# A hybrid two-layer block on one core: a fourth raw weight buffer, a deeper weight queue and a reordered mixer

## The chip, the cores and the metric

The kernel runs on one core of a Trainium2 chip. The metric is the device time of one execution in microseconds (us). Before the change it is 1276.12 us, the median of 3 runs (1275.52 to 1276.19).

## The reference

Two layers, each of them a feed-forward block, a mixer block and a second feed-forward block on 256 tokens of width 1024, all in float32, and a last norm:

```python
for l in range(DEPTH):                                   # 2 layers
    x = x + 0.5 * swiglu_ffn(rms_norm(x, ffn1_norm[l]), ffn1_w1[l], ffn1_w2[l])   # 1024 -> 2*2816 -> 1024
    h = rms_norm(x, mix_norm[l])
    proj = h @ w_in[l]                                   # split into gm_u, gm_v, r_q .. r_g, n_q, n_kv, n_g
    y_a = gmlp_mixer(gelu(gm_u), gelu(gm_v), ...)        # layer norm, causal 128x128 mix over tokens
    y_b = retention_mixer(r_q, r_k, r_v, r_g, ...)       # 4 heads, decayed scores, group norm, silu gate
    y_c = nsa_mixer(n_q, n_kv, n_g, ...)                 # compressed, selected and window attention, 8 heads
    g_a, g_b, g_c = split(sigmoid(h @ w_merge_gate[l] + b_merge_gate[l]), 3)
    x = x + (g_a * (y_a @ w_branch_out[l, 0]) + g_b * (y_b @ w_branch_out[l, 1])
             + g_c * (y_c @ w_branch_out[l, 2])) @ w_o[l]
    x = x + 0.5 * swiglu_ffn(rms_norm(x, ffn2_norm[l]), ffn2_w1[l], ffn2_w2[l])
return rms_norm(x, final_norm)
```

## The kernel before

**Weights.** All weights lie in one DRAM tensor in the order of their use and come as pieces of at most 128 x 1024 floats (512 KB). `issue` (L197) makes a piece: a DMA on SyncE's queue (SP) into one of three `raw` buffers (L199), a cast on ScalarE (ACT) to the high half `hl` (L210), and a subtraction that makes the low half (L214) on VectorE (DVE), of which GpSimd (POOL) takes the last part, as `pool_lo` says. `hl` has four buffers. `piece` (L220) hands a piece to TensorE (PE) and issues those up to `AHEAD` = 2 pieces further on. Each product is made of three matmuls: high by high, high by low, low by high.

**Order.** PE's order is the program's. The other engines and SP each have a queue in order, which the framework's scheduler fills from the program by its own model of time. Side work (norms, attention, retention, the gated MLP) is written as generators: `yield 3.5` means "go on when 3.5 us of modelled matmul time have passed on PE", `yield has("vr")` means "go on when this has been emitted". `run_sides` looks at them after every third matmul or so.

**Start.** `ffn` of layer 0 loads x in quarters, each followed by a quarter of the first piece (`xload`, L425). `norm_tile` makes the high half of x on ACT (L314) and the low half on DVE (L315). `square` sums the squares on POOL (L323, L329, L333). `gate_pool` (L250) holds POOL back until a piece is split. `norm_end` (L349) has PE sum over partitions (after `WAIT_FIRST` = 16.5), POOL take the power (L346), and PE spread the result, R, over the partitions; the outputs of the first four column blocks wait in PSUM for R (L398), two of them in the two `mm` banks.

**Mixer.** `feat` and `tok` run through w_in: compressed keys, keys (`f_k`), values, queries (`f_q`), retention's queries and keys, gv, retention's values (`f_vr`, evacuated by ACT at L949), gate features u and g. From `f_q` on, `pool_lo` = 5: POOL makes 3/8 of each low half. `f_q` writes the queries' high half with ACT and their low half with DVE into `ql` (L935), and two DMAs on SP (L937, L938) move that to the other 64 partitions. `mirror` (L532) does the same for keys with two DMAs on SP (L536, L537). `hidden` runs a compression piece of 8 short matmuls between the query and retention blocks. `retention` (L741) makes decayed scores, waits for `vr` and `cmp`, then 1.5, and makes the second stage (L757 on): scores by values, of which the third and fourth head need the second half of `f_vr`. `gmlp` (L837) and `unit` (L616, attention of one query tile and key group) follow as sides. `loads` (L465) brings the mixer's constants, on SP.

Of the kernel before, what the change touches and what calls it, by code (L numbers as in the profile page):

```python
# [7 lines left out]
F32 = mybir.dt.float32  # L8
# [17 lines left out]
AHEAD = 2  # L26
# [12 lines left out]
WAIT_FIRST = 16.5  # L39
# [3 lines left out]
WAIT_SCORE = 4.5  # L43
WAIT_PT = 3.5
WAIT_CB = 8.0
WAIT_GN = 3.5
WAIT_LN = 6.0
WAIT_GMLP = 10.0
# [12 lines left out]
def tile_hybrid_block(  # L61
# [26 lines left out]
    const.tile([128, 24], F32, tag="align", name="align")  # L88
# [36 lines left out]
    def pms():  # L125
        return ps.tile([128, 512], F32, tag="ms", name=nm("ms"), bufs=2)

# [122 lines left out]
    def gate_pool(t):  # L250

        G.tensor_copy(small(1), t.bitcast(F32)[:, 0:1])

# [36 lines left out]
    mhalf = const.tile([128, 4], F32, tag="mhalf", name="mhalf")  # L290
    G.memset(mhalf, -0.5)
    S.activation(mhalf[:, 2:4], mhalf[:, 0:2], AF.Copy)
# [27 lines left out]
    def square(st, k):  # L320
        last = st["n"] == 7 and st["i"] > 0
# [56 lines left out]
    def ffn(st, nxt, first=False, load=None):  # L378
# [26 lines left out]
        for j in range(NJ):  # L405
# [11 lines left out]
            if j == 0 and not first:  # L417
                wks = [piece(8, 128), piece(8, 128)]
                p = (p, psc())
                yield from mm_pair([p[0][:, 0:256], p[1][:, 0:256]], wks, st["a"])  # L420
            for half in range(2):
                if j == 0 and not first:
                    break
                if first and j == 0 and half == 0:
# [5 lines left out]
                    gate_pool(queue[1][7][:, 1])  # L430
# [34 lines left out]
    def loads(l):  # L465

        yield 0.0
        if l == 0:
            C["alibi"] = const.tile([128, 8, 256], BF, tag="alibi", name="alibi")
            tmp = s8(F32)  # L470
            for i in range(2):
                nc.sync.dma_start(tmp[:, i], c_alibi[:, 4 * i:4 * i + 4])
                G.tensor_copy(C["alibi"][:, 4 * i:4 * i + 4], tmp[:, i])
            C["decay"] = ctile([128, 4, 256], c_decay, nc.sync, "decay")
            C["ccmp"] = ctile([128, 2, 2, 4, 2, 16], c_cmp, nc.sync, "ccmp")
            V.tensor_tensor(out=fold, in0=ident[:, 0:30], in1=ident[:, 30:60], op=ALU.add)
            C["vm"] = ctile([128, 8], c_vm, nc.sync, "vm")
        P["lng"] = ctile([128, 2, 512], lnp[l:l + 1].to_broadcast([128, 2, 512]), nc.sync, "lng")
        P["bsb"] = ctile([128, 4, 128], bs[l:l + 1].to_broadcast([128, 4, 128]), nc.sync, "bsb")
        P["wt"] = ctile([128, 4, 128], wst[:, l], nc.sync, "wt")  # L480
        for g in range(4):
            G.tensor_tensor(out=P["wt"][:, g], in0=P["wt"][:, g], in1=tri, op=ALU.mult)
        P["w2c"] = ctile([128, 192], cw2[:, l], nc.sync, "w2c")
        P["pos"] = ctile([128, 2, 16], cpos[:, l], nc.sync, "pos")
        P["gnc"] = ctile([128, 2, 4], gn[:, l], nc.sync, "gnc")
# [752 lines left out]
```

## Time and profile before

| | |
|---|---|
| median of 3 runs | 1276.12 us |
| profiled execution, own time | 1276.49 us |
| its span, first to last instruction | 1274.7 us |
| PE busy | 1251.5 us (98%) |
| DVE busy | 975.6 us (77%) |
| ACT busy | 718.7 us (56%) |
| POOL busy | 497.0 us (39%) |
| mean granted clock of PE | 0.992 |
| moved by DMA | 231.51 MB, 182 GB/s on average |

The span is 1.8 us short of the execution's own time; a prediction made on the span carries over with that difference. PE's busy time has modelled ends of matmuls, so a stretch can be full and still run slow, by the clock or by late weights. PEld is the weight load that overlaps the matmuls.

### The profile page before, as it was taken

To read this page: it belongs to the slowest core of one execution; us is meant where nothing else is said; L and a number is where in the kernel's file an instruction comes from. 1 tells how busy PE (TensorE), PEld (TensorE's weight loads), DVE (VectorE), ACT (ScalarE), POOL (GpSimd) and SP (SyncE) were. 2 spreads that over 40 slices of the span, in tenths; PEclk is the share of its full clock that TensorE was granted. 3 is DMA by queue.
4 is the path that set the end of the run, shared out by engine and by line. 5 is a ranking of instruction groups with operands and counts; after the bars stand their busy time and mean duration, and the time that the engine had idled before them with its cause. 6 is when DMAs were issued, how large, how long until landed. Compare 5 with 4: busy or idle time off the path is not lost.

```text
span 1274.7 us, 22825 instructions
## 1 busy us (share of the span) xinstructions
PE 1251.5 (98%) x8440; PEld 1150.0 (90%) x8440; DVE 975.6 (77%) x1671; ACT 718.7 (56%) x1217; POOL 497.0 (39%) x455
## 2 busy tenths in 40 slices
PE   9999999999999999999999999999999999999997
PEld 8888889899999988888898888998999999888886
DVE  5888776679876788887778887766997769788764
ACT  5566544556765556664456664455676645566642
POOL 4533121664355743331303321236534568133222
PEclk8999999999999999999999999999999999999999
DMA  7755565755454565555655556676445455655562
GB/s 240 247 193 184 185 190 185 228 166 173 133 166 154 165 195 186 194 187 190 188 190 188 186 191 193 186 212 200 145 135 159 154 158 175 195 185 189 186 193 92
DMA packets 70303, 231.51 MB, mean 182 GB/s; under 512 B 9392, under 2 KB 12080, under 8 KB 70192
## 3 DMA queue, kind: packets, MB, share of 16 engines
q1 hardware_dynamic: 70048, 230.03, 56.7%
q8 instruction: 66, 1.08, 0.4%
q14 instruction: 45, 0.37, 0.1%
q10 hardware_dynamic: 144, 0.03, 0.0%
HBM read 225.80 MB, written 1.05 MB: 178 GB/s over the span
## 4 chain that ended last, share of the span: by engine, by line
PE 83%; DVE 7%; DMA 4%; ACT 3%; issue 2%; POOL 1%; SPq 0%; POOLq 0%; DVEq 0%; ACTq 0%
PE mm L139 57%; PE sc L139 22%; DMA raw<-in_w_dram 3%; DVE hl L214 2%; ACT hl L210 2%; PE ms L139 2%; POOL hl L214 1%; PE o L139 1%; PE sc L149 1%; DVE xhl L315 1%; DMA gnorm<-in_norms_dram 0%; PE ms L149 0%; DVE P L645 0%; DVE t L563 0%; DVE t L459 0%
## 5 line engine op out<-in xcount | busy, mean ns | idle before, releaser
L214 DVE TENSOR_TENSOR hl<-raw,hl 128x896 fp32r<-128x896 f32 (+6 forms) x437 | 486.8, 1116 | 170.0 <-ACT hl L210 166.8
L210 ACT CAST hl<-raw 128x1024 fp32r<-128x1024 f32 (+3 forms) x437 | 443.3, 1016 | 260.3 <-PE mm L139 155.8
L139 PE MATMUL mm<-xhl,hl 128*128 128x256 f32 (+1 forms) x3784 | 570.8, 306 | 3.6 <-DVE hl L214 1.1
L139 PEld LDWEIGHTS mm<-xhl,hl 128*128 128x128 f32 x3784 | 512.0, 191 | 39.3 <-DVE hl L214 2.3
L214 POOL TENSOR_TENSOR hl<-raw,hl 128x128 fp32r<-128x128 f32 (+2 forms) x288 | 350.3, 1218 | 495.1 <-ACT hl L210 473.7
L139 PE MATMUL mm<-s,hl 128*128 128x512 f32 (+1 forms) x1880 | 296.6, 318 | 0.0
L139 PEld LDWEIGHTS mm<-s,hl 128*128 128x128 f32 x1880 | 266.9, 188 | 26.9
L139 PE MATMUL sc<-xhl,hl 128*128 128x256 f32 (+1 forms) x1560 | 275.7, 328 | 0.0
L139 PEld LDWEIGHTS sc<-xhl,hl 128*128 128x128 f32 x1560 | 230.4, 188 | 28.7
L329 POOL TENSOR_TENSOR sq<-x 128x256 f32<-128x256 f32 x43 | 30.1, 703 | 135.6 <-DVE x L374 135.6
L391 ACT COPY t<-sc 128x256 f32<-128x256 f32 x81 | 30.2, 373 | 77.2 <-PE sc L139 77.1
L391 ACT COPY t<-mm 128x256 f32<-128x256 f32 x81 | 30.0, 371 | 59.8 <-PE mm L139 59.8
L139 PE MATMUL mm<-hl,xhl 128*128 128x256 f32 (+1 forms) x432 | 61.9, 291 | 1.4 <-DVE hl L214 1.1
L333 POOL TENSOR_TENSOR acc<-acc,sq 128x256 f32<-128x256 f32 x43 | 60.8, 1414 | 2.5
L139 PEld LDWEIGHTS mm<-hl,xhl 128*128 128x128 f32 x432 | 55.2, 190 | 4.8 <-issue 1.9
L393 DVE TENSOR_TENSOR t<-t,R 128x512 f32<-128x512 f32 x81 | 56.9, 702 | 2.8
L399 ACT ACTIVATE t<-t 128x256 f32<-128x256 f32 x88 | 36.8, 418 | 29.0 <-DVE t L393 26.4
L392 DVE TENSOR_TENSOR t<-sc,t 128x256 f32<-128x256 f32 x81 | 34.3, 424 | 22.7 <-ACT t L391 22.6
L650 ACT ACTIVATE P<-P,small 128x128 f32<-128x128 f32 (+1 forms) x64 | 28.6, 449 | 33.6 <-DVE small L648 33.5
L374 DVE SCALAR_TENSOR_TENSOR x<-mm,x 128x256 f32<-128x256 f32 x84 | 35.5, 422 | 15.8 <-PE mm L139 14.5
L315 DVE SCALAR_TENSOR_TENSOR xhl<-x,gnorm,xhl 128x256 fp32r<-128x256 f32 x48 | 41.6, 877 | 5.2 <-ACT xhl L314 5.2
L392 DVE TENSOR_TENSOR t<-mm,t 128x256 f32<-128x256 f32 x81 | 34.3, 423 | 6.5 <-ACT t L391 1.3
(179 smaller groups left out, 853.5 us busy)
## 6 DMA issues: line engine op xcount, KB each, us to landing
raw<-in_w_dram SPq DMA_DIRECT2D x389, 512.0 KB, 3.5
raw<-in_w_dram SPq DMA_DIRECT2D x32, 384.0 KB, 3.3
raw<-in_w_dram SPq DMA_DIRECT2D x4, 420.0 KB, 3.1
x<-in_x_dram SPq DMA_DIRECT2D x4, 256.0 KB, 4.2
raw<-in_w_dram SPq DMA_DIRECT2D x8, 128.0 KB, 3.7
lng<-in_lnp_dram SPq DMA_DIRECT2D x2, 512.0 KB, 5.1
s<-in_c_alibi_dram SPq DMA_DIRECT2D x2, 512.0 KB, 5.5
ks<-ks SPq DMA_DIRECT2D x4, 256.0 KB, 5.5
```

The source lines that it names most:

```text
L139: nc.tensor.matmul(o, lhsT=lhsT, rhs=rhs, start=start, stop=stop)
L210: S.copy(hi[:, s_], raw[:, s_])
L214: e.tensor_tensor(out=lo[:, a:b], in0=raw[:, a:b], in1=hi[:, a:b].bitcast(F32), op=ALU.subtract)
L315: V.scalar_tensor_tensor(st["l"][:, k], xs[k], g, st["h"][:, k].bitcast(F32), op0=ALU.mult, op1=ALU.subtract)
L329: (V if last else G).tensor_tensor(out=q, in0=xs[k], in1=xs[k], op=ALU.mult)
L333: (V if last else G).tensor_tensor(out=st["acc"], in0=st["acc"], in1=q, op=ALU.add)
L374: V.scalar_tensor_tensor(xs[d], p[:, i:i + 256], 0.5, xs[d], op0=ALU.mult, op1=ALU.add)
L391: S.copy(t3[:, n], p[n][:, 256:512])
L392: V.tensor_tensor(out=t3[:, n], in0=p[n][:, 0:256], in1=t3[:, n], op=ALU.add)
L393: V.tensor_tensor(out=t3, in0=t3, in1=R2, op=ALU.mult)
L399: S.activation(u[:, 0:256], t[:, 0:256], AF.Silu)
L650: S.activation(Pt[:, b, 0:nk], Pt[:, b, 0:nk], AF.Exp, bias=mx[:, b:b + 1], accum_out=sm[:, b:b + 1])
```

## The change

A fourth `raw` buffer; `AHEAD` = 3, with `ahead=2` where two pieces are taken at once. Room for it: `ql` goes (the low half of the queries is written by DVE straight to the other partitions, without DMAs), and `vc` moves into a part of `tb` that retention has read by then. The first norm's squares go to ACT and their sums to DVE, `gate_pool` goes, `WAIT_FIRST` is 13, and the first activation on ACT is a Silu. `loads` pauses 4.0 between its constants. The copies of `mirror` move from SP's queue to POOL's. `pool_lo` falls to 5 only after `f_kr`. Retention's second stage waits 3.5 instead of 1.5; `gmlp` waits for `yn` and 11 instead of 10; the second attention unit waits 4.5 instead of 2.5 before its transposes. `soon()` is a context that does nothing, `align` (96 bytes a partition) goes, and some of the new names in the list of constants are used nowhere.

```diff
-AHEAD = 2
+AHEAD = 3
-WAIT_FIRST = 16.5
+WAIT_FIRST = 13.0
+WAIT_LOAD = 4.0
-WAIT_GMLP = 10.0
+WAIT_GMLP = 11.0
+WAIT_VR = 3.5
+WAIT_P = (2.5, 4.5, 2.5, 2.5)
...
-    const.tile([128, 24], F32, tag="align", name="align")
...
+    def soon():
+
+        return nullcontext()
...
-        raw = ring.tile([128, SLOT], F32, tag="raw", name=nm("raw"), bufs=3)
+        raw = ring.tile([128, SLOT], F32, tag="raw", name=nm("raw"), bufs=4)
...
-    S.activation(mhalf[:, 2:4], mhalf[:, 0:2], AF.Copy)
+    S.activation(small(2), mhalf[:, 0:2], AF.Silu)
...
     def square(st, k):
-        last = st["n"] == 7 and st["i"] > 0
+        if st["i"] == 0:
+            q = st["acc"] if k == 0 else act.tile([128, 256], F32, tag="sq", name=nm("sq"), bufs=2)
+            S.activation(q, xs[k], AF.Square)
+            if k:
+                V.tensor_tensor(out=st["acc"], in0=st["acc"], in1=q, op=ALU.add)
+            st["n"] += 1
+            return
+        last = st["n"] == 7
...
-                wks = [piece(8, 128), piece(8, 128)]
+                wks = [piece(8, 128), piece(8, 128, ahead=2)]
...
-                    gate_pool(queue[1][7][:, 1])
...
             C["decay"] = ctile([128, 4, 256], c_decay, nc.sync, "decay")
+            yield WAIT_LOAD
...
-        VC = t2("vc", 1).rearrange("p (j c) -> p j c", j=4)
+        VC = tb[:, 0:2].rearrange("p a b -> p (a b)").rearrange("p (j c) -> p j c", j=4)
...
-            nc.sync.dma_start(f[64:128, :, 0, lo:hi], f[0:64, :, 0, lo:hi])
-            nc.sync.dma_start(f[0:64, :, 1, lo:hi], f[64:128, :, 1, lo:hi])
+            G.dma_start(f[64:128, :, 0, lo:hi], f[0:64, :, 0, lo:hi])
+            G.dma_start(f[0:64, :, 1, lo:hi], f[64:128, :, 1, lo:hi])
...
-            yield 2.5
+            yield WAIT_P[2 * qt + g]
...
             yield has("vr", "cmp")
-            yield 1.5
+            yield WAIT_VR
...
+            ev.add("yn")
             yield 7.0
...
-            yield lambda: 0 in yh and "gv" in ev
+            yield lambda: 0 in yh and "gv" in ev and "yn" in ev
             yield WAIT_GMLP
...
-            ql = act.tile([128, 2, 256], F32R, tag="ql", name=nm("ql"), bufs=1)
             for v in range(2):
-                s_ = slice(v * 64, v * 64 + 64)
+                s_, o_ = slice(v * 64, v * 64 + 64), slice(64 - v * 64, 128 - v * 64)
                 S.copy(QS[s_, v, j:j + 2], q3[s_])
-                V.tensor_tensor(out=ql[s_], in0=q3[s_], in1=QS[s_, v, j:j + 2].bitcast(F32), op=ALU.subtract)
-            f = QS.bitcast(F32)
-            nc.sync.dma_start(f[64:128, 0, j:j + 2], ql.bitcast(F32)[0:64])
-            nc.sync.dma_start(f[0:64, 1, j:j + 2], ql.bitcast(F32)[64:128])
+                V.tensor_tensor(out=QS[o_, v, j:j + 2], in0=q3[s_], in1=QS[s_, v, j:j + 2].bitcast(F32), op=ALU.subtract)
...
-        pool_lo[0] = MIX_SPLIT
         yield from feat(4, f_q, after=0)
         yield from feat(2, f_qr, after=4)
         yield from feat(2, f_kr, after=6)
+        pool_lo[0] = MIX_SPLIT
```

## Rows read from the trace of the kernel before

**Rows 1.** Windows of 25 us: length, busy and count by engine, clock, DMA share, GB/s
```profile
0.00:25.00 25.00, 22.13 (x128) 20.18 (x129) 15.29 (x22) 11.81 (x23) 13.73 (x24) 0.86 0.71 238
...
100.00:125.00 25.00, 25.00 (x143) 21.66 (x143) 20.65 (x31) 15.06 (x27) 7.87 (x10) 1.00 0.55 186
...
850.00:875.00 25.00, 23.01 (x185) 21.79 (x184) 18.25 (x21) 12.43 (x16) 16.08 (x11) 1.00 0.75 230
```

**Rows 2.** Waits of PE, whole run: us in total, times, longest
```profile
PE ms L139 <- ACT s L949: 3.8, 2, 1.9
```

**Rows 3.** Chain that ended last, whole run: start, us, what
```profile
12.58 5.71 PE mm L139 x32
...
71.36 2.83 PE mm L139 x16
...
469.07 2.77 PE mm L139 x16
```

**Rows 4.** Groups of DVE from 4 to 17 us: busy, mean ns, idle before
```profile
L315 DVE SCALAR_TENSOR_TENSOR xhl<-x,gnorm,xhl 128x256 fp32r<-128x256 f32 x8 | 6.3, 823 | 5.2 <-ACT xhl L314 5.2
L214 DVE TENSOR_TENSOR hl<-raw,hl 128x256 fp32r<-128x256 f32 x8 | 4.4, 583 | 0.0
```

**Rows 5.** Timeline at the second norm: start, us, instruction
```profile
202.87 0.40 ACT L327 ACTIVATE sq<-x 128x256 f32<-128x256 f32 x1
...
203.73 0.48 DVE L315 SCALAR_TENSOR_TENSOR xhl<-x,gnorm,xhl 128x256 fp32r<-128x256 f32 x1
204.12 0.42 DVE L333 TENSOR_TENSOR acc<-acc,sq 128x256 f32<-128x256 f32 x1
```

**Rows 6.** Timeline at the first norm
```profile
18.76 1.60 POOL L333 TENSOR_TENSOR acc<-acc,sq 128x256 f32<-128x256 f32 x1
...
34.29 1.28 ACT L399 ACT_TABLE_LOAD   x1
...
37.20 3.07 PE L139 MATMUL mm<-xhl,hl 128*128 128x512 f32 x16 [0.98 <-DVE t L398]
```

**Rows 7.** Sum of the sixteen 2 us windows from 220 to 252 us
```profile
sum 32.00, PE 30.62 PEld 29.18 DVE 22.73 ACT 18.02 POOL 19.75; mean PE 1.91 PEld 1.82 DVE 1.42 ACT 1.13 POOL 1.23
```

**Rows 8.** Chain that ended last, 205 to 300 us
```profile
229.86 0.48 SPq L938
...
230.45 3.99 DMA raw<-in_w_dram
...
234.54 1.06 ACT hl L210
...
235.67 1.66 POOL hl L214
...
237.35 4.09 DMA raw<-in_w_dram
...
257.46 2.87 PE mm L139 x24
```

**Rows 9.** Groups of POOL and of DVE, 220 to 262 us
```profile
L214 POOL TENSOR_TENSOR hl<-raw,hl 128x384 fp32r<-128x384 f32 x10 | 16.2, 1630 | 25.2 <-ACT hl L210 24.6 <-DVE ql L935 0.6
...
L214 DVE TENSOR_TENSOR hl<-raw,hl 128x640 fp32r<-128x640 f32 x10 | 10.8, 1087 | 6.5 <-ACT hl L210 6.4
...
L214 DVE TENSOR_TENSOR hl<-raw,hl 128x1024 fp32r<-128x1024 f32 x1 | 1.2, 1223 | 0.0
```

**Rows 10.** Windows around retention's second stage, both layers
```profile
274.00:278.00 4.00, 4.00 (x36) 4.00 (x34) 4.00 (x14) 2.64 (x6) 3.64 (x5) 1.00 0.55 181
...
281.40:285.60 4.20, 3.76 (x19) 3.77 (x20) 3.63 (x11) 3.13 (x6) 3.57 (x3) 0.60 0.38 119
...
905.60:910.00 4.40, 3.88 (x21) 3.88 (x22) 3.76 (x12) 3.21 (x7) 3.68 (x3) 0.65 0.27 73
```

**Rows 11.** Timeline of the compressed keys' copy and its first reader
```profile
263.85 0.63 SPq L536 DMA_DIRECT2D ks<-ks  x1
...
269.80 0.43 PE L139 MATMUL sc<-ks,xhl 128*128 128x288 f32 x2
```

More of the change, by code (lines that the diff above doesn't have):

```diff
@@ L1 @@
-from contextlib import ExitStack
+from contextlib import ExitStack, nullcontext
 import concourse.bass as bass
@@ L38 @@
 WAIT_POW = 1.0
-WAIT_FIRST = 16.5
+WAIT_FIRST = 13.0
+WAIT_LOAD = 4.0
+EARLY = 120
+WAIT_POW2 = 2.5
 WAIT_FOLD = 3.0
@@ L42 @@
 WAIT_COPY = 0.5
-WAIT_SCORE = 4.5
-WAIT_PT = 3.5
+WAIT_SCORE = (4.5, 4.5)
+WAIT_PT = (3.5, 3.5)
 WAIT_CB = 8.0
 WAIT_GN = 3.5
+WAIT_OB = 1.5
 WAIT_LN = 6.0
-WAIT_GMLP = 10.0
+WAIT_GMLP = 11.0
+WAIT_VR = 3.5
+WAIT_P = (2.5, 4.5, 2.5, 2.5)
 def _pieces():
@@ L248, in mm_chunks @@
             yield
-    def gate_pool(t):
-        G.tensor_copy(small(1), t.bitcast(F32)[:, 0:1])
     def mm_wide(o, wk, ak, first, last):
@@ L682, in unit @@
                 pl = PL[n % 2]
-                S.copy(ph, pt)
-                V.tensor_tensor(out=pl, in0=pt, in1=ph.bitcast(F32), op=ALU.subtract)
+                with soon():
+                    S.copy(ph, pt)
+                    V.tensor_tensor(out=pl, in0=pt, in1=ph.bitcast(F32), op=ALU.subtract)
                 PT[n] = (ph, pl)
@@ L692, in unit @@
             t = t2()
-            S.copy(t[own], o[oth])
-            V.tensor_tensor(out=os[qt][own], in0=o[own], in1=t[own], op=ALU.add)
+            with soon():
+                S.copy(t[own], o[oth])
+                V.tensor_tensor(out=os[qt][own], in0=o[own], in1=t[own], op=ALU.add)
             ev.add(f"u{qt}{g}")
@@ L723, in cmp_branch @@
                 mm(p[:, j * 128:j * 128 + 128], lhsT=VC[:, j], rhs=ct, start=True, stop=True)
-            V.tensor_tensor(out=o, in0=o, in1=p, op=ALU.add)
             qs = slice(qt * 128, qt * 128 + 128)
             o3 = o.rearrange("p (j t) -> p j t", j=4)
-            S.copy(yh[2][:, :, qs], o3)
-            V.tensor_tensor(out=yl[2][:, :, qs], in0=o3, in1=yh[2][:, :, qs].bitcast(F32), op=ALU.subtract)
+            with soon():
+                V.tensor_tensor(out=o, in0=o, in1=p, op=ALU.add)
+                S.copy(yh[2][:, :, qs], o3)
+                V.tensor_tensor(out=yl[2][:, :, qs], in0=o3, in1=yh[2][:, :, qs].bitcast(F32), op=ALU.subtract)
             ev.add(f"yc{qt}")
@@ L860, in feat @@
                     p = (p[:, 0:256], psc()[:, 0:256])
-                    wks = [piece(8, 128), piece(8, 128)]
+                    wks = [piece(8, 128), piece(8, 128, ahead=2)]
                     yield from mm_pair(p, wks, a)
@@ L990, in gates @@
             t = t2("tg", 2)
-            V.tensor_tensor(out=t.rearrange("p (a b) -> p a b", a=2), in0=p.rearrange("p (a b) -> p a b", a=2), in1=R2(), op=ALU.mult)
+            with soon():
+                V.tensor_tensor(out=t.rearrange("p (a b) -> p a b", a=2), in0=p.rearrange("p (a b) -> p a b", a=2), in1=R2(), op=ALU.mult)
             for n, i in enumerate(idx):
@@ L1013, in mixer @@
             u = t2()
-            V.scalar_tensor_tensor(u, t_prev, 1.0, p, op0=ALU.add, op1=ALU.mult)
+            with soon():
+                V.scalar_tensor_tensor(u, t_prev, 1.0, p, op0=ALU.add, op1=ALU.mult)
             G.tensor_tensor(out=ms[d // 4][:, d % 4], in0=u[:, 0:256], in1=u[:, 256:512], op=ALU.add)
@@ L1057, in mixer @@
         p = (pmm()[:, 0:256], psc()[:, 0:256])
-        yield from mm_pair(p, [piece(8, 128), piece(8, 128)], mk)
+        yield from mm_pair(p, [piece(8, 128), piece(8, 128, ahead=2)], mk)
         for d in range(2):
```

14 lines of the change are left out of this document (10 added, 4 removed).

## The prediction, made before the changed kernel was run

> **What bounds the kernel now.** I read the windows of the whole run first, then PE's waits, then the chain. In the feed-forward stages PE is full at full clock (25.00 of 25.00 us) while every other engine has room [rows 1]. The chain there is PE alone, one half piece-pair after the other at 2.77 us [rows 3]. Nothing on other engines shortens that, so all that the change can win lies where PE isn't full or not at full clock: the first 37 us, the stretch of small pieces in each mixer (the window from 850 shows PE at 23.01 and its weight loads at 21.79 of 25), and one wait in each mixer that is the longest in the list, 3.8 us in two times [rows 2]. Each is costed by itself; as PE is the chain on both sides of each, what PE wins there comes off the end one to one.
>
> **The start.** PE cannot go faster here than DVE makes low halves of x and of the first pieces: per quarter of the first piece two of L315 and one of L214. They take 823 and 583 ns [rows 4], 2.23 us a quarter. The same L315 takes 0.48 us at the second norm, where POOL is idle, and a DVE operation on 128x256 there 0.42 [rows 5]. So what POOL does beside it, the squares, costs DVE 0.85 us a quarter, 3.4 us over four. With the squares on ACT a quarter costs 1.38. The price: eight squares of 0.40 on ACT, 3.2 us, and seven additions of 0.42 on DVE, 2.9 us [rows 5]. In program order they come after the splits of the first pieces, and their sum is wanted only by the norm's column sums, so I put most of them behind the splits. If all ran ahead of them, 2.9 of the 3.4 would be gone again. The fourth raw buffer also lets the DMA of the fourth piece go about when the third has gone, and not when the first is split. In the first 25 us the mean granted clock is 0.86 [rows 1]: PE ran part of it at 1.2 GHz after a stretch of short bursts, and the run of 32 matmuls from 12.58 took 5.71 us [rows 3], where 120 ns each (24 in 2.87 [rows 8]) would make 3.8. Fewer gaps can bring the clock back earlier, at most these 1.9. Bounds: 0.5 (additions in the way) to 5.3 (3.4 and the clock's 1.9). I take 3.0, the DVE time won less a little, since the data's landing will then bind in places.
>
> The wait at 37.20 for R, 0.98 us [rows 6], goes: the column sums come 3.5 modelled us earlier, and POOL's last addition used to end at 20.36 [rows 6], far ahead of them, so there is room for a sum that is made by DVE. Bounds 0 to 1.0; I take 1.0. The table load of 1.28 us moves to the start, where ACT waits for the first DMA anyway; at 34.29 it was hidden as well. `gate_pool` is one short POOL operation; nothing waited for it.
>
> **Constants.** Spreading them costs and gives nothing that I can see: no PE wait falls between 12.58 and 37.20 but the one above, and the readers are in the mixer, after 200 us. If a weight DMA was late for their sake, DMA share 0.71 in the first window [rows 1] says it had room.
>
> **The stretch of small pieces.** From 220 to 252 the weight loads, which elsewhere in this stretch are without gaps, are busy 29.18 of 32.00 [rows 7]: 2.8 us lost to late weights. Layer 1 loses 25 − 21.79 = 3.2 [rows 1]. The chain shows why: a raw buffer goes round in DMA 3.99, cast 1.06, POOL's low half 1.66, and the next DMA starts at 237.35, 6.9 us after the last at 230.45 [rows 8]. With three buffers that is a piece per 2.3 us. PE wants 12 pieces of 24 matmuls and 4 of 8 here, 12 × 2.87 + 4 × 0.96 = 38.3 us for 16 [rows 8], 2.4 us a piece on average, but less where a short piece is among them, and nothing is left over. Ahead of the DMA at 230.45 SP was also held by the copy of the queries (L938, 0.48) and by DVE's work for it [rows 8]. After: no copies of queries (their DVE work stays, it only writes elsewhere), and the low half by DVE alone at 1.22 for 1024 columns, against 1.09 with POOL's 1.63 beside it [rows 9]. So DVE pays only 0.14 us a piece for what POOL no longer does. The round becomes 3.99 + 1.06 + 1.22 = 6.3 us, and with four buffers a piece per 1.6. Bytes allow it: 512 KB in 1.6 us is 330 GB/s at most, while only 2.4 us a piece are asked. Some of the lost weight-load time is around float32 matmuls and stays; I take 2.3 of 2.8 and 2.7 of 3.2, together 5.0, bounds 2.0 (another wait for low halves behind DVE's other work) and 6.0. `AHEAD` by itself moves only the order in the queues; what is ahead is set by the buffers.
>
> **Retention's second stage.** PE waits 1.9 us for ACT's evacuation L949 in each layer [rows 2], 3.8 in sum, and straight after that the granted clock is 0.60 over 4.2 us and 0.65 over 4.4 [rows 10]: part of it at 1.2 GHz. At the neighbour's 36 PE instructions in 4.00 us, the 19 in 3.76 busy us should have taken 2.1 and the 21 in 3.88 2.3; so the clock costs 1.65 + 1.55 = 3.2. Two modelled us more, some 18 matmuls of u's features whose weights are split by then, cover the 1.9. The evacuation itself is not made earlier. Without the long gap I expect no fall of the clock. Together 7.0; bounds 0 (the evacuation, in ACT's queue behind the exponentials of attention, slips by the same 2 us) and 7.0. What is late next: group norm and `gmlp` (its 11 and `yn`) by 2 to 3 us, both far ahead of the output products; the last part of retention is released by `sg`, which stays.
>
> **Moved or without price.** `mirror` on POOL: see the rival. `VC` in `tb` and the second unit's 4.5 change only when something is emitted; I count nothing for them. `soon` is nothing. Addresses move by 96 bytes; no row prices that. The nearest is a spread that I can't explain: the same half pair takes 2.83 in the first feed-forward block and 2.77 later [rows 3], 2.0 us over the 36 half pairs of that block (18 of the 22 columns are wide). I take 0, bounds −2 and +2.
>
> **Sum.** 3.0 + 1.0 + 5.0 + 7.0 = 16.0. Against it I set 1.0 for the copy of compressed keys on POOL's queue (half a microsecond a layer, between 0 and the rival's price). Net 15.0. The execution's own time is 1276.5 (span 1274.7 and 1.8 around it), 0.4 above the median of the runs: 1276.5 − 15.0 − 0.4 = 1261.
>
> **Rivals.** *Half of it.* The retention wait stays because ACT is the late one and its queue slips along: 7.0 less, 1268. Or the late weights stay since DVE, now with all low halves, is late: 5.0 less, 1266. For the first speaks that DVE, on which ACT's exponentials hang, is busy 4.00 of 4.00 us just before [rows 10]; against both, that over the whole stretch DVE and ACT have room on average (22.73 and 18.02 of 32 us [rows 7]).
>
> *The compressed keys' copy comes late.* SP sent it at 263.85 and PE read it at 269.80 [rows 11], 5.9 us later. On POOL it stands behind low halves of 1.6 to 1.8 us [rows 9], and POOL's own issue has no row. If the copy lands 8 us after it is ready, PE waits 2.1 a layer, and with a fall of the clock such as after the 1.9 us wait [rows 10] 3.7, 7.4 in all, of which 1.0 is counted: 1267. The rule of the Trainium skill that speaks against this edit ("SBUF — State Buffer", § the "DVE blocks DMA" trap) says that a DMA issued from POOL needs POOL to write its descriptors and stalls while DVE holds their shared port, about 0.6 us growing to 3.1. By that page, an estimate, 2.5 us more would still fit into the margin; no run here shows it yet.
>
> *Slower: a cast at the head of ACT's queue.* With pieces three ahead, the cast of a piece may stand in ACT's queue before the evacuation of a finished pair and wait for an `hl` buffer, of which there are still four. The evacuation must free an `mm` bank within two half pairs, 5.5 us. A cast that waits one half pair, 2.77, and takes 1.06, leaves 1.7 us for about 1.6 us of evacuation (ACT and DVE twice, about 0.4 each, as the 128x256 rows show [rows 5]). It decides when the wait is 0.1 us longer; at 0.3 us for each of some 84 pairs it costs 25 us: 1276 − 15 + 25 = 1286. Against it: `hl` has as many buffers as before, so no cast can run earlier than it did, and PE is full today with the same limit [rows 1].
>
> *The change does nothing:* all four stalls return elsewhere, 1274 to 1278.
>
> **How the numbers follow.** Forecast (1256 to 1266): 0.56. Half of it or the late copy (1266 to 1273): 0.26. Nothing (1274 to 1278): 0.06. Slower by the cast or a like head-of-queue wait: 0.09. More than the sum (under 1256, the unexplained 2 us, the clock at the start): 0.03. About 0.2%, 2.5 us, is what a measurement of this kernel can tell from no change: faster 0.85, same 0.05, slower 0.10. The range for 8 in 10 runs from 1254 to 1272.
>
> **What would show it.** Start: L315 near 0.48 us, and PE's first unbroken run some 3 us earlier; the wait for L398 gone. Small pieces: PE's waits for `hl` under 1 us a layer and weight loads near full. Retention: no wait for L949 of 1.9 us, clock 1.00 around it. Copy: no PE wait for `ks`. The forecast is wrong if additions or squares stand before splits at the start, if L949 slips, or if the feed-forward windows are no longer full.

## The result: slower by 0.6%, where 1.2% faster was forecast

The changed kernel takes 1283.22 us in the median of 4 runs (1281.51 to 1284.61). The kernel before took 1275.82 us beside it. The ratio is 1.006, with an interval from 1.0042 to 1.0078. The forecast of 1261.0 us is 22 us off, and the time lies outside its range.

Each of the four stalls that the forecast counted was removed. The time came out elsewhere. This is the list of PE's waits after; the columns are us in total, times and the longest.

```profile
PE o L148 <- DVE xhl L703: 4.6, 4, 1.9
PE o L148 <- ACT ph L702: 3.8, 2, 1.9
PE sc L148 <- ACT s L748: 3.4, 2, 1.7
PE sc L148 <- DVE s L749: 2.7, 2, 1.4
...
PE mm L148 <- ACT hl L219: 0.8, 2, 0.4
```

Line numbers are now 5 to 22 higher: L702 and L703 were L683 and L684, L748 and L749 were L727 and L728. Retention's wait [rows 2] is no longer in the list. Weights make PE wait 0.8 us in all. In their place stand 8 us for copies of attention's transposed scores and 6 us for the last sums of the compressed branch.

Both traces have the same 8440 PE instructions, so the run can be cut at the same matmuls in every kernel. These are the lengths in us between the starts of such matmuls, worked out from the traces. "Start" runs from PE's first matmul to the first wide one; "wide" is the run of 512-column matmuls (every other one has 256 columns) in a feed-forward block; what lies between two such runs, with the mixer in it, is "mixer". The labels are those of the experiments below. Each row is one execution, and the executions of one kernel differ, by up to 7 us (e8_before_vr: 1279.0 to 1286.4); the one of after, 1281.9, is one of its two faster ones.

```
kernel               start  wide 1   mixer 0  wide 2  wide 3  wide 4  mixer 1
before               36.22  155.89   270.27   169.52  169.52  169.52  270.40
after                30.26  154.86   275.38   170.66  171.66  171.66  272.24
e1_vr                30.57  153.85   269.14   170.66  171.66  171.66  267.20
e2_p                 31.10  153.85   272.51   171.66  171.66  171.66  272.62
e6_vr_raw3           31.12  153.85   268.39   171.66  171.66  171.66  267.23
e8_before_vr         36.77  155.89   271.88   169.52  169.52  169.52  272.73
e10_vr_squares       37.68  154.94   269.87   171.66  171.66  171.66  267.36
e12_vr25             30.67  153.85   272.53   171.66  171.66  171.66  272.44
e5_before_noalign    37.08  155.89   268.01   169.52  169.52  169.52  270.11
e14_before_pad       36.53  154.94   270.50   171.66  171.66  171.66  269.72
e13_vr_pad           30.18  155.17   269.12   172.03  172.03  172.03  267.31
e15_after_pad        30.43  155.18   274.81   172.03  172.03  172.04  274.32
e17_vr_place         30.30  155.48   270.51   170.20  170.20  170.20  267.83
e18_after_place      30.69  155.48   274.73   170.20  170.20  170.20  275.66
```

From before to after the start is 6.0 shorter, the wide stages 4.4 longer and the mixers 6.9 longer, which gives 5.4, the difference of the spans (1280.1 and 1274.7). The forecast had 4.0 shorter, nothing, and 11.0 shorter. The mixers alone are 18 us off.

**What came as forecast.** First the groups of DVE in the first microseconds, which answer to [rows 4]:

```profile
L320 DVE SCALAR_TENSOR_TENSOR xhl<-x,gnorm,xhl 128x256 fp32r<-128x256 f32 x8 | 3.5, 481 | 5.0 <-ACT xhl L319 5.0
L223 DVE TENSOR_TENSOR hl<-raw,hl 128x256 fp32r<-128x256 f32 x8 | 3.2, 414 | 0.0
L330 DVE TENSOR_TENSOR acc<-acc,sq 128x256 f32<-128x256 f32 x7 | 2.9, 414 | 0.1
```

The splits fell from 823 to 481 ns and from 583 to 414 ns. Then four windows of after; the columns are those of [rows 1].

```profile
0.00:25.00 25.00, 23.10 (x168) 22.18 (x169) 16.97 (x33) 17.24 (x34) 1.42 (x9) 1.00 0.84 283
214.00:246.00 32.00, 32.00 (x261) 31.11 (x260) 26.53 (x37) 18.23 (x30) 1.98 (x3) 1.00 0.83 253
844.00:869.00 25.00, 25.00 (x209) 24.77 (x209) 22.36 (x32) 16.48 (x27) 1.25 (x2) 1.00 0.73 234
...
278.40:283.00 4.60, 4.60 (x41) 4.60 (x40) 4.05 (x18) 2.52 (x5) 2.05 (x2) 1.00 0.55 175
```

The clock at the start is 1.00 in place of 0.86. In the stretches that lost 2.8 and 3.2 us to late weights [rows 1, 7] PE is now full, and the weight loads are 0.9 and 0.2 us short of it. Around retention's second stage the clock is 1.00 where it was 0.60 [rows 10]. The copy of the compressed keys on POOL made nobody wait, as these lines of the timeline show, two of POOL and one of PE:

```profile
254.26 0.60 POOL L554 DMA_DIRECT2D ks<-ks  x1 [0.90 <-DVE ks L563]
254.85 0.58 POOL L555 DMA_DIRECT2D ks<-ks  x1
...
259.82 0.42 PE L148 MATMUL sc<-ks,xhl 128*128 128x288 f32 x2
```

From issue to reader are 5.6 us, and PE doesn't wait.

**Where it was lost: the first attention unit.** This is the timeline of after, first PE, then DVE, then POOL, then ACT. A bracket is the idle time before and what ended it.

```profile
284.88 0.33 PE L158 MATMUL sc<-sq,P 128*128 128x128 f32 x1 [0.28 <-DVE P L672]
284.97 4.20 PE L148 MATMUL mm<-xhl,hl 128*128 128x256 f32 x33
291.06 0.57 PE L148 MATMUL o<-ph,xhl 128*128 128x512 f32 x1 [1.89 <-ACT ph L702]
293.50 0.80 PE L148 MATMUL o<-xhl 128*128 128x512 f32 x1 [1.87 <-DVE xhl L703]
...
286.69 0.17 DVE L791 TENSOR_SCALAR small<-small 128x4 f32<-128x4 f32 x1
287.99 0.41 DVE L796 TENSOR_SCALAR s<-ms,small,small 128x128 f32<-128x128 f32 x1 [1.13 <-POOL small L792]
288.32 0.68 DVE L982 TENSOR_TENSOR t<-mm,R 128x512 f32<-128x512 f32 x1
...
292.76 0.68 DVE L703 TENSOR_TENSOR xhl<-sc,ph 128x512 fp32r<-128x512 f32 x1
...
286.94 1.01 POOL L792 TENSOR_TENSOR small<-small,mhalf 128x4 f32<-128x4 f32 x1 [1.06 <-DVE small L791]
...
289.03 0.63 ACT L469 ACTIVATE t<-t 128x512 f32<-128x512 f32 x1 [2.99 <-DVE t L982]
...
290.44 0.56 ACT L702 CAST ph<-sc 128x512 fp32r<-128x512 f32 x1
```

Read it backwards from PE's wait at 291.06. The transposes are done by 285.2. Their copy L702 stands in ACT's queue behind the gelu of u (L469), which waits 2.99 us for the scaling of u (L982). That stands in DVE's queue behind the second group norm (L788 to L796), which itself waits for POOL's power. The group norm is what the change put off. It now falls between the transposes and their copies. With the second stage at its old place (e1 below) the norm's last step is done when the transposes end, and the copy follows 1.4 us after them in place of 5.2:

```profile
285.16 0.40 DVE L796 TENSOR_SCALAR s<-ms,small,small 128x128 f32<-128x128 f32 x1
285.48 0.60 PE L158 MATMUL sc<-sq,P 128*128 128x128 f32 x4
287.52 0.56 ACT L702 CAST ph<-sc 128x512 fp32r<-128x512 f32 x1
```

Just behind the first of the two waits, from 291.3, the granted clock of after is at its lower level, 1.2 GHz, for 6.8 us; the second wait lies in that time.

**And the end of the attention.** PE first, then DVE and ACT, after:

```profile
400.75 1.05 PE L148 MATMUL ms<-sct,s 128*128 128x128 f32 x8
401.55 1.32 PE L148 MATMUL mm<-xhl,hl 128*128 128x256 f32 x9
404.57 0.39 PE L148 MATMUL sc<-s,hl 128*128 128x256 f32 x1 [1.70 <-ACT s L748]
406.31 0.86 PE L148 MATMUL sc<-s,hl 128*128 128x256 f32 x5 [1.35 <-DVE s L749]
...
404.77 1.48 DVE L749 TENSOR_TENSOR s<-ou,s 128x512 fp32r<-128x512 f32 x1
...
402.95 1.04 ACT L219 CAST hl<-raw 128x1024 fp32r<-128x1024 f32 x1 [1.43 <-PE mm L148]
403.90 0.61 ACT L748 CAST s<-ou 128x512 fp32r<-128x512 f32 x1
```

Between the last product of the compressed branch and its first reader the order has only 9 matmuls, 1.3 us. The kernel before had 27 there, 3.5 us:

```profile
406.37 3.48 PE L139 MATMUL mm<-xhl,hl 128*128 128x256 f32 x27
...
410.43 2.75 PE L139 MATMUL sc<-s,hl 128*128 128x256 f32 x21 [0.47 <-DVE s L728]
```

A part of the wait is the weights' cast (L219), which stands ahead of L748 in ACT's queue: the sum that L748 reads is done at 403.04, and L748 starts at 403.90, 0.9 us later. In the kernel before a cast stood there as well (L210 at 407.05, L727 at 408.00), behind which the 27 matmuls left room.

### The profile page after: what moved, and what is told of

The parts are those of the page before. It is cut to its first block, busy times and chain, and to the rows that moved or that the text cites. A ratio compares the mean times of both kernels' runs of the same rounds, so it can differ in the third digit from the quotient of the medians.

```text
span 1280.1 us, 22627 instructions
## 1 busy us (share of the span) xinstructions
PE 1252.2 (98%) x8440; PEld 1151.2 (90%) x8440; DVE 991.3 (77%) x1678; ACT 713.5 (56%) x1224; POOL 441.3 (34%) x423
## 4 chain that ended last, share of the span: by engine, by line
PE 85%; POOL 5%; DVE 5%; issue 2%; ACT 2%; DMA 0%; POOLq 0%; DVEq 0%; ACTq 0%
PE mm L148 58%; PE sc L148 23%; PE ms L148 2%; POOL hl L223 2%; POOL acc L345 1%; DVE hl L223 1%; PE o L148 1%; ACT hl L219 1%; POOL sq L341 1%; PE sc L158 1%; DVE t L470 0%; POOL s L854 0%; ACT P L668 0%; POOL small L792 0%; POOL s L855 0%
## 5 line engine op out<-in xcount | busy, mean ns | idle before, releaser
L223 DVE TENSOR_TENSOR hl<-raw,hl 128x896 fp32r<-128x896 f32 (+6 forms) x437 | 497.8, 1141 | 174.8 <-ACT hl L219 173.2
L219 ACT CAST hl<-raw 128x1024 fp32r<-128x1024 f32 (+3 forms) x437 | 442.1, 1016 | 307.5 <-PE mm L148 198.6
L223 POOL TENSOR_TENSOR hl<-raw,hl 128x128 fp32r<-128x128 f32 (+2 forms) x264 | 302.8, 1148 | 509.8 <-ACT hl L219 503.7
L341 POOL TENSOR_TENSOR sq<-x 128x256 f32<-128x256 f32 x36 | 25.0, 694 | 137.4 <-DVE x L386 137.4
L414 DVE TENSOR_TENSOR s<-t,s 128x256 fp32r<-128x256 f32 x88 | 56.7, 645 | 0.0
L345 POOL TENSOR_TENSOR acc<-acc,sq 128x256 f32<-128x256 f32 x36 | 51.5, 1430 | 2.0
L412 DVE TENSOR_TENSOR t<-t,t 128x256 f32<-128x256 f32 x88 | 37.3, 425 | 0.6 <-ACT t L411 0.5
```

The source lines that it names most:

```text
L219: S.copy(hi[:, s_], raw[:, s_])
L223: e.tensor_tensor(out=lo[:, a:b], in0=raw[:, a:b], in1=hi[:, a:b].bitcast(F32), op=ALU.subtract)
L341: (V if last else G).tensor_tensor(out=q, in0=xs[k], in1=xs[k], op=ALU.mult)
L345: (V if last else G).tensor_tensor(out=st["acc"], in0=st["acc"], in1=q, op=ALU.add)
L412: V.tensor_tensor(out=u[:, 256:512], in0=u[:, 0:256], in1=t[:, 256:512], op=ALU.mult)
L414: V.tensor_tensor(out=l4[:, j % 4], in0=u[:, 256:512], in1=h4[:, j % 4].bitcast(F32), op=ALU.subtract)
```

## The experiments

All numbers are medians with the ratio to the kernel before, run beside them. "After" is the changed kernel, 1283.2 us.

**e1_vr: after, retention's second stage where it was.**
```
-WAIT_VR = 3.5
+WAIT_VR = 1.5
```


> The changed kernel with retention's second stage back at 1.5 (everything else as changed). Theory (place of the side work): the waits for the first unit's ph and low half (1.9 + 1.9 us a layer, and the fall of the clock behind them, some 3.4 us in layer 0 and 1.7 in layer 1) come from group norm's DVE and POOL work standing 2 us later, in front of them; they shrink to under 1 us a layer, and retention's wait for its values comes back with up to 1.9 us. Net 2 to 6 us faster than the changed kernel's 1283. Rival (depth of the queue: casts and low halves stand before the evacuations): these waits stay at 3.5 us or more a layer and retention's wait is added: 1283 to 1287.

1270.60 us, 0.9966 (0.9955 to 0.9978): faster than both kernels, and by more than the theory's 2 to 6 us under after. This single number is worth 12.6 us. Its waits of PE from 261 to 320 us, and the end of its attention in the timeline, with 21 matmuls where after has 9:

```profile
PE mm L148 <- DVE tg L1010: 2.8, 1, 2.8
PE ms L148 <- ACT s L967: 2.0, 1, 2.0
```

```profile
397.40 2.76 PE L148 MATMUL mm<-xhl,hl 128*128 128x256 f32 x21
400.15 0.38 PE L148 MATMUL sc<-s,hl 128*128 128x256 f32 x1
400.87 2.99 PE L148 MATMUL sc<-s,hl 128*128 128x256 f32 x23 [0.34 <-DVE s L749]
```

**e2_p: after, the second unit's wait where it was.**
```
-WAIT_P = (2.5, 4.5, 2.5, 2.5)
+WAIT_P = (2.5, 2.5, 2.5, 2.5)
```


> The changed kernel with the second attention unit's pause back at 2.5. Theory (place of the side work): the end of attention moves 2 us of matmuls forward, so PE's waits for the last compressed outputs (1.7 + 1.35 us a layer near 403 and 1034) fall under 1 us a layer as in the kernel before (0.5), and the fall of the clock in layer 0 goes; 4 to 7 us faster than the changed kernel. Rival (depth of the queue): the cast that stands before the copy on ACT keeps the wait at 2.5 us or more; within 1.5 us of the changed kernel.

1280.32 us, 1.0041 (1.0026 to 1.0056), 2.9 us less than after and between the two expectations. The wait on L748 is gone and L749 is down to 0.9 us, but the gates' evacuation L1010 now makes PE wait 2.7 us.

**e3_ahead2: after with two pieces ahead.**
```
-AHEAD = 3
+AHEAD = 2
```


> The changed kernel with two pieces ahead instead of three, still four raw buffers. Theory (place of the side work): the waits of the first unit (3.8 us a layer) and of the last compressed outputs (3.0 a layer) stay, within 2 us of the changed kernel's 1283, and weights are no later, as the buffers set what is ahead. Rival (depth of the queue): these waits fall by more than half, 5 us or more faster.

1279.29 us, 1.0027 (1.0013 to 1.0041). L702, L748 and L749 still cost 9.4 us. Depth is not the main cause, though it adds some 4 us, between the two expectations.

**e4_align: after with the 96 bytes back ahead of the weights' buffers.**
```
+    const.tile([128, 24], F32, tag="align", name="align")
```


> The changed kernel with the 96 bytes back in front of the buffers, so that the weights' halves start at a multiple of 128 bytes again; nothing else. Theory (addresses): the wide stages of the four feed-forward blocks return to the kernel before's 169.5 us in blocks 2 to 4 (from 170.7, 171.7, 171.7), some 4 to 5 us faster in sum, mixers as in the changed kernel. Rival (the pace of a wide stage is set by how it was entered, by chance): blocks take either pace as before, differing from run to run, within 2 us of the changed kernel in the median.

1284.61 us, 1.0074 (1.0052 to 1.0096); wide stages as in after. This shift does nothing.

**e5_before_noalign: before without the 96 bytes.**
```
-    const.tile([128, 24], F32, tag="align", name="align")
```


> The kernel before with the 96 bytes ahead of its buffers left out, and nothing else. Open question: the 16-matmul passes of the feed-forward's wide part go at 169.5 us a stage in the kernel before and at 170.7 to 171.7 us in the changed one. If the place of the buffers in a partition sets that pace, this kernel takes the changed kernel's stages: 2 to 6 us over the kernel before (1278 to 1282 us). If the pace comes from how the weights' pieces arrive (four raw slots, three pieces ahead), the stages stay at 169.5 us and the time within 1 us of the kernel before.

1275.20 us, 0.9998 (0.9982 to 1.0013); wide stages exactly those of before.

**e6_vr_raw3: e1 with three raw slots and two pieces ahead.**
```
-AHEAD = 3
+AHEAD = 2
...
-        raw = ring.tile([128, SLOT], F32, tag="raw", name=nm("raw"), bufs=4)
+        raw = ring.tile([128, SLOT], F32, tag="raw", name=nm("raw"), bufs=3)
```


> The changed kernel with retention's second stage put back (1.5) and with three raw slots and two pieces ahead, so with all of the change but the weights' buffering and retention's place. Theory A (buffering sets the pace of the wide stages): the stages of the feed-forward come back to 169.5 us, 4 to 6 us less, and what the late weights cost comes back too, 0 to 5 us more: 1266 to 1271 us. Theory B (buffering has nothing to do with the pace): stages stay at 170.7 to 171.7 us, and the late weights of 220 to 252 us and 850 to 875 us come back: 1272 to 1276 us.

1272.72 us, 0.9979 (0.9964 to 0.9994). Both theories fall in part: the wide stages stay slow, and the late weights don't come back (below, at e16). The fourth slot and the third piece are together worth some 2 us.

**e7_vr_p: e1 and e2 together.**
```
-WAIT_VR = 3.5
+WAIT_VR = 1.5
-WAIT_P = (2.5, 4.5, 2.5, 2.5)
+WAIT_P = (2.5, 2.5, 2.5, 2.5)
```


> The changed kernel with both waits put back: retention's second stage at 1.5 and the attention's second unit at 2.5. If the compressed branch's last outputs still come too early behind their transposes when retention stands where it stood, this takes away what is left of those waits (0.7 us on L749 in the kernel with 1.5 alone): 1268 to 1270 us. If instead the whole attention, ended 2 us earlier, meets other late work (the score's tanh gates, as with 2.5 alone, 1.7 us on L1010), it is 1270 to 1274 us.

1271.35 us, 0.9966 (0.9953 to 0.9979): no better than e1. PE waits 4.6 us for L702 and L703 again, in place of the 4.5 for L1010 in e1.

**e8_before_vr: before, with retention's second stage alone put off.**
```
             yield has("vr", "cmp")
-            yield 1.5
+            yield 3.5
```


> The kernel before with retention's second stage put off alone: 3.5 in place of 1.5. My theory: the place of this stage costs the changed kernel its 12 us, since the group norm's chain comes between the transposes of the first attention unit and their copies; then the kernel before, too, grows by 5 to 12 us (1281 to 1288 us), with the wait on L949 gone and waits of the matmuls for the copies of the transposes in its place. Rival: the later place is good as such and hurts only with the changed kernel's other moves (gmlp behind the norm, weights' copies); then it is 0 to 7 us faster (1269 to 1276 us).

1281.67 us, 1.0049 (1.0030 to 1.0068). The place costs the kernel before 6 us, too, by another wait than was expected, 8.4 us in the two layers. This is PE's line in the timeline of the first:

```profile
301.18 1.22 PE L139 MATMUL ms<-wt,s 128*128 128x128 f32 x4 [4.17 <-DVE s L775]
```

It is the gmlp that waits here. Its matmul doesn't read what L775 writes; it writes into a PSUM buffer that the late group norm still reads.

**e9_gn_late: after, the second norm's last step on DVE emitted 5 later.**
```
                 yield WAIT_GN
+                if it:
+                    ev.add("yn")
+                    yield 5.0
...
-            ev.add("yn")
-            yield 7.0
+            yield 2.0
```


> The changed kernel, retention's second stage where the change puts it (3.5), but the second group norm's last step on VectorE (L796, which waits for GpSimd's power) is emitted 5 later; its matmuls, the gmlp's matmuls and retention's transposes stay where they were emitted. Theory: L796 waits 1.1 us on VectorE just ahead of the scaling of u (L982) and of the copies of the first attention unit's transposes (L702, L703), and that makes the two waits of 1.9 us in each layer and the half clock behind them; then these waits fall to under 1 us each and the kernel is 4 to 10 us faster than the changed one (1273 to 1279 us). Rival: the copies are late for the scaling of u and its gelu, whatever L796 does; then the two waits stay at 1.5 us or more and the time stays at 1281 to 1284 us.

1281.63 us, 1.0039 (1.0026 to 1.0053). The wait on L703 at the first unit fell from 1.9 to 0.5 us or less. That on L702 stayed at 1.9. The first of the four steps of L796 still stood just ahead of the scaling of u and waited 1.13 us for POOL, though it was emitted later (only PE's queue is in the order of emission); the edit took away only what stood behind it. The rival's time holds. So this run doesn't show that the norm's step makes the wait on L702; that rests on the timeline above and on e1.

**e10_vr_squares: e1 with the first squares and sums back on GpSimd.**
```
-WAIT_FIRST = 13.0
+WAIT_FIRST = 16.5
...
-        if st["i"] == 0:
-            q = st["acc"] if k == 0 else act.tile([128, 256], F32, tag="sq", name=nm("sq"), bufs=2)
-            S.activation(q, xs[k], AF.Square)
-            if k:
-                V.tensor_tensor(out=st["acc"], in0=st["acc"], in1=q, op=ALU.add)
-            st["n"] += 1
-            return
-        last = st["n"] == 7
+        last = st["n"] == 7 and st["i"] > 0
```


> The kernel with retention's second stage at 1.5, and the first norm's squares and sums back as they were (GpSimd alone, and the wait of 16.5). The weights' four slots, the early table load and all else of the change stay. Theory: the 6 us that the start gained come from the squares and their sums; the first wide matmul goes from 30.6 back to 35 to 36 us and the time to 1274 to 1277 us. Rival: half or more comes from the rest (weights three pieces ahead, the table, no gate on GpSimd): 31 to 33.5 us and 1271 to 1273.5 us.

1279.84 us, 1.0022 (1.0012 to 1.0032). The start is 37.7 us, 7.1 more than in e1. The group of DVE and the first window:

```profile
L320 DVE SCALAR_TENSOR_TENSOR xhl<-x,gnorm,xhl 128x256 fp32r<-128x256 f32 x8 | 6.7, 881 | 5.2 <-ACT xhl L319 5.2
```

```profile
0.00:25.00 25.00, 21.42 (x115) 18.95 (x116) 17.46 (x23) 12.87 (x24) 12.14 (x23) 0.80 0.72 233
```

The squares, their sums and the shorter wait, which this edit puts back together, are the whole gain of the start. Part of it is the clock, 0.80 here and 1.00 in e1's first window: 10.2 us at the lower level, worth 5.1 at most. The time is over both expectations: the first two wide stages are 2.1 us longer than in e1, too, at the same distance of buffers (below).

**e11_no_yn: after, with its gmlp as before.**
```
-            yield lambda: 0 in yh and "gv" in ev and "yn" in ev
+            yield lambda: 0 in yh and "gv" in ev
...
-WAIT_GMLP = 11.0
+WAIT_GMLP = 10.0
```


> The changed kernel with its gmlp as before: it does not wait for the group norm's event, and its wait is 10 in place of 11. Retention's second stage stays at 3.5. My prediction counted this part at nothing. Theory: with retention late, the gmlp's first matmul finds both of its PSUM buffers held by the group norms and waits some 4 us in each layer, as in the kernel before with 3.5 (there 4.2 us, twice); 1283 to 1290 us. Rival: the gmlp's place makes no difference here: 1281 to 1284 us.

1284.36 us, 1.0060 (1.0045 to 1.0075).

```profile
PE ms L148 <- DVE s L796: 11.6, 2, 5.8
PE o L148 <- ACT ph L702: 2.4, 2, 1.2
```

The gmlp waits 5.8 us a layer, more than expected, and in return the waits on L748 go and L703 falls to 0.8. The wait changes its place, not its size.

**e12_vr25: after, half way.**
```
-WAIT_VR = 3.5
+WAIT_VR = 2.5
```


> The changed kernel with retention's second stage at 2.5, half way between 1.5 (1270.6 us) and 3.5 (1283.2 us). If the slip matters by its size (each us later pushes the group norm's chain a us further between the transposes and their copies), it comes half way: 1274 to 1279 us, with about 1 us left on ACT's rows of retention (L967) in each layer. If one order of instructions decides (the group norm ahead of or behind the scaling of u on VectorE), it is like one of the two: 1269 to 1272 us, or 1281 to 1285 us.

1280.14 us, 1.0034 (1.0024 to 1.0044), in none of the three expected ranges and nearer to 3.5 than to 1.5. L967 costs 1.0 a layer, and five more waits of 0.5 to 1.0 us in layer 0 take the rest. L748 and L749 cost 6.1 us as in after.

**e13_vr_pad and e15_after_pad: e1 and after, with 32 bytes between the weights' buffers and the activations'.**
```
+    act.tile([128, 8], F32, tag="pad", name="pad")
```


> The kernel with retention's second stage at 1.5, and 32 bytes between the weights' buffers and the activations', so that their distance in a partition is a multiple of 128 bytes as in the kernel before (there 32768, now 33408, in the changed kernel 33376). Theory: this distance sets the pace of the wide matmul pairs; the feed-forward's stages come back to 169.5 us from 170.7 to 171.7, in all 4 to 6 us: 1264.5 to 1267.5 us. Rival: the distance has nothing to do with it; the stages stay at 170.7 to 171.7 and the time at 1270 to 1272 us.

> The changed kernel with the 32 bytes of e13 and nothing else. Theory: 3 to 6 us less than the changed kernel, from the feed-forward's stages alone (1277 to 1280 us), and its waits in the mixers stay as they were. Rival: 1281 to 1285 us.

1273.58 us, 0.9980 (0.9971 to 0.9990), and 1286.40 us, 1.0081 (1.0064 to 1.0097). The wide stages are 172.03 us in both: the theory that a multiple of 128 bytes brings the old pace back falls. But the pace did change, and alike in two kernels.

**e14_before_pad: before, with its 96 bytes moved to that place.**
```
-    const.tile([128, 24], F32, tag="align", name="align")
+    act.tile([128, 24], F32, tag="pad", name="pad")
```


> The kernel before with its 96 bytes moved from ahead of the weights' buffers to between them and the activations' (distance 32864, 96 over a multiple of 128, as in the changed kernel). Theory: the feed-forward's three later stages go from 169.5 to about 171 us, the first from 155.9 to about 154.5: 3 to 5 us more, 1278 to 1281 us. Rival: they stay, and the time is within 1 us of the kernel before.

1282.34 us, 1.0052 (1.0034 to 1.0070). The wide stages are those of the changed kernel's slower pace to 0.1 us (154.94, 171.66 three times). Nothing but the place of buffers differs from e5, which has 155.89 and 169.52.

**e17_vr_place and e18_after_place: e1 and after with the old distance of 32768 bytes.**
```
-    S.activation(small(2), mhalf[:, 0:2], AF.Silu)
+    S.activation(mhalf[:, 4:6], mhalf[:, 0:2], AF.Silu)
```


> The kernel with retention's second stage at 1.5; the early activation that loads the table writes into the constant's spare columns and no longer into a small tile, so that the small tiles' buffers come after the activations' and the distance is 32768 bytes as in the kernel before. Theory: stages of the feed-forward at 169.5 us (from 170.7, 171.7, 171.7) and the first at 154 to 156 us: 3 to 5 us less, 1265.5 to 1268 us. Rival: the pace hangs on more than this distance; stages at 170.5 to 172 us and 1269.5 to 1273.5 us.

> The changed kernel with that one line alone. Theory: 3 to 5 us less than the changed kernel by the same stages, 1278 to 1280 us, and the waits in the mixers as they were. Rival: 1281 to 1285 us.

(The changed kernel has `mhalf` 8 columns wide in place of 4, which the diff above leaves out; this edit writes to the spare ones.) 1269.17 us, 0.9948 (0.9937 to 0.9960), the fastest of all; and 1282.88 us, 1.0054 (1.0039 to 1.0069). The wide stages are 155.48 and three times 170.20 in both, so neither expectation holds for them: 170.20 lies between 169.52 and after's pace. In e18 they are together 2.8 us shorter than in after, and the time is not, since its mixers are 2.8 us longer, with 20.5 us at 1.2 GHz in place of 13.7. One link of the chain in the second block, of after, e14, e17 and e13 in this order; all are half a pair of pieces, as in [rows 3]:

```profile
470.07 2.80 PE sc L148 x16
```

```profile
468.72 2.80 PE mm L139 x16
```

```profile
468.53 2.77 PE mm L148 x16
```

```profile
466.86 2.81 PE mm L149 x16
```

At the old distance the first 42 of the 61 links of a later block have their old pace again (2.77); the rest, which read other buffers, take 2.80 to 2.82, so e17 is 0.7 us a stage slower than before.

**e16_raw3_pool: e6 with GpSimd's low halves at their old place.**
```
+        pool_lo[0] = MIX_SPLIT
         yield from feat(4, f_q, after=0)
         yield from feat(2, f_qr, after=4)
         yield from feat(2, f_kr, after=6)
-        pool_lo[0] = MIX_SPLIT
```


> The kernel with retention at 1.5, three raw slots and two pieces ahead, and GpSimd's share of the low halves from the queries on, as before (the change starts it after retention's keys). No query copies on SP's queue. Theory: GpSimd's low halves of 1.7 us are what made the weights late from 220 to 252 us; the weight loads fall from 31.1 to 29 to 30 of 32 us there, and the kernel grows by 2 to 5 us over the one without (1272.7): 1274 to 1278 us. Rival: the query copies on SP's queue were it; then the weight loads stay at 31 of 32 us and the time within 1.5 us of 1272.7.

1277.66 us, 1.0015 (1.0003 to 1.0026), 5 us above e6. The stretch of small pieces in e6 and then in e16:

```profile
215.00:247.00 32.00, 32.00 (x260) 31.11 (x260) 23.88 (x35) 18.62 (x26) 4.15 (x3) 1.00 0.71 239
```

```profile
216.00:248.00 32.00, 30.41 (x240) 28.69 (x238) 22.12 (x31) 17.53 (x22) 22.26 (x15) 1.00 0.71 224
```

The weight loads fall from 31.11 to 28.69 us. GpSimd's low halves in this stretch made the weights late. Three slots are enough without them, and the copies of the queries on SP, which are gone in both, were not the cause.

## Why the prediction was wrong

**The step that failed is retention's second stage**, "Together 7.0; bounds 0 ... and 7.0", with what followed: "What is late next: group norm and `gmlp` ... both far ahead of the output products". What is late next are not their readers but whoever stands behind them on DVE and ACT. So the premise that "what PE wins there comes off the end one to one" failed here. With this stage at its old place and all else changed (e1), the mixers are 4.3 us shorter than before, against 4.0 forecast for the weights less the copy. The stage's own move then costs 11.3 us (after less e1: 6.2 and 5.0) where 7.0 were to be won.

Most of the 11.3 can be added up. PE's waits from retention to the end of the first units' products are 4.9 us in after and 4.8 in e1 in layer 0, 4.5 and 3.9 in layer 1: hardly a difference, 0.7. The waits at the end of the attention are 6.1 us in after and 0.7 in e1: 5.4. The clock is at 1.2 GHz for 13.7 us of the mixers in after, of which PE waits 1.9 anyway, and for 3.4 in e1, of which it waits 0.2: half of the difference of the rest is 4.3, an upper bound. Together that is at most 10.4; 0.9 is not accounted for.

Why the waits stay can be read from three windows, of after, of e1 and of before:

```profile
262.00:294.00 32.00, 27.96 (x225) 26.86 (x224) 29.36 (x95) 20.20 (x44) 19.53 (x18) 0.96 0.45 149
```

```profile
261.00:288.00 27.00, 24.95 (x210) 24.76 (x209) 26.21 (x90) 17.54 (x42) 18.20 (x16) 1.00 0.48 159
```

```profile
270.00:302.00 32.00, 30.09 (x240) 29.90 (x239) 30.26 (x98) 21.46 (x46) 20.02 (x17) 0.95 0.49 165
```

DVE (the third busy time after the length) is busy 29.4 of 32 us, 26.2 of 27 and 30.3 of 32. It has next to no room in any of the three. The reading is that in this stretch DVE is the bound, not PE, and that PE's wait for L949 was the place where DVE and ACT caught up. What the runs show is that the wait, taken away there, comes back at a later result behind DVE: L702 and L703 in after, the gmlp's buffer in e8 and e11. Likewise, when the waits at the end of the attention are taken away, L1010 grows from 0.4 to 2.7 us (e2). That DVE's load is the reason, and not the order in its queue alone, is not shown, since no run took work off DVE there. The prediction saw DVE at 4.00 of 4.00 [rows 10], and used it only for a rival that halves the gain. It set aside that reading by the average over 32 us of another stretch [rows 7]. That no value below zero was in the bounds was the second mistake.

All that the prediction named as signs of being right came: the faster splits, full small pieces, no wait for L949 and clock 1.00 around it, no wait for `ks`. All of them look at the places that were changed, and none at what comes behind.

**"I count nothing"** for the second unit's 4.5 was wrong as well: 2 us later, and with retention's slip, the attention runs into its fixed readers. Either edit undone (e1, e2) removes most of it. With retention at 1.5 the 4.5 costs nothing that can be measured: 1270.60 with it (e1), 1271.35 without (e7).

**Addresses, "I take 0, bounds −2 and +2":** 4.4 us. e14 shows that the place of buffers alone can make this pace. By the kernels' allocations the distance from the first weight buffer to the activations' is 32768 bytes in before (four `hl` buffers) and 33376 in after (with 19 small buffers of 32 bytes between). It is not the removed 96 bytes that did it (e4, e5). The early table load did the larger part: its output is the first small tile, and so the small tiles' buffers come to lie between. With that one line undone (e18) the wide stages get back 2.8 of the 4.4; what makes the other 1.6 is open.

**The start, 4.0:** 6.0. The mechanism was right (e10); the clock, in the bound with 1.9, should have been in the value: before was at 1.2 GHz for 6.8 us of its start, after not at all. The wait for R went too.

**Late weights, 5.0:** the size is right (the weight loads won 1.9 and 3.0 us in the two stretches), the cause half wrong. It was POOL's low halves (e16: 4.9 us over e6). "With four buffers a piece per 1.6" hardly mattered (e6).

**Rivals.** The cast at the head of ACT's queue did not come in the feed-forward pairs, where it was priced (PE waits 0.8 us in all for `hl` by ACT). One does stand ahead of L748 (above), but as well with two pieces ahead (e3: L219 at 400.34, L748 at 401.29), so it isn't the deeper queue's. "A like head-of-queue wait", at 0.09, is the branch nearest to what came: L702 behind the gelu of u. The late copy did not come: POOL's issues took 0.60 and 0.58 us, and PE didn't wait. The Trainium skill ("SBUF — State Buffer", § "A bandwidth-pool intuition that's wrong (but worth ruling out)") gives a DMA issued from POOL about 0.62 us alone and about 3.1 us beside a DVE copy that holds the port shared with POOL. No such stall shows in this trace, but it is no test of that rule: DVE was idle beside most of the first issue, and beside the second it made a subtraction (from 254.66), not a copy.

Open: which pair of buffers sets the pace, and by what. The second part of a wide block reads other buffers and kept a slow pace at the old distance (e17). Kernels with the same distance differ by 1.0 us in the first or the second wide stage, too: after has 154.86 and 170.66, e1 153.85 and 170.66, e2 153.85 and 171.66.

## What to carry to other kernels

Before a wait of PE is moved, look which engine is busy through it. If that engine is full over the next ten or twenty microseconds, the wait may be its time to catch up, and can come back at a later result, perhaps with a fall of the clock. And an operation that is put off is late not only for its readers but for all that stands behind it in its engine's queue.

Signs of being right that look only at the changed places can all come true while the time gets worse; name one for what comes behind, too.

A new small buffer ahead of large ones can cost as much as a stall. After an edit that seems to touch no hot loop, compare the duration of one link of the chain in that loop.

## What the hardware showed that was not expected

The same 16 matmuls (512 and 256 columns in turn) took 2.77, 2.80 or 2.81 us in the first part of the second block, by the place of buffers and without a wait in the trace. e14 and e5 differ in nothing else. e13 and e15 agree to 0.01 us a stage, e17 and e18 too; the kernels at after's distance agree in the third and fourth wide stages (171.66) and differ by 1.0 us in the first two.

A gap of 2.0 us in PE is followed by a fall of the clock in some kernels and not in others. These are windows from 269 to 275 us in e1 and then in e6, each with the same gap of 2.0 us in it, which ends at 271.2 and at 271.7 (the clock is the number behind the five busy times, 1.00 and 0.84):

```profile
269.00:275.00 6.00, 3.96 (x34) 3.82 (x32) 5.28 (x14) 3.89 (x9) 5.33 (x4) 1.00 0.32 85
```

```profile
269.00:275.00 6.00, 3.95 (x27) 3.76 (x26) 5.28 (x12) 4.00 (x9) 5.44 (x5) 0.84 0.19 72
```
